# Modulation rows for all partitions: read back from a copy in DRAM instead of built by TensorE and ScalarE

## The chip, the cores and the metric

The kernel runs on one core of a Trainium2 chip. The metric is device microseconds from start to end of one execution. Engines are named as in the profile: PE is TensorE, DVE is VectorE, ACT is ScalarE, POOL is GpSimd and SP is SyncE. SP computes nothing here; it issues the weight loads.

## What is computed

Two layers of a diffusion backbone over 512 tokens of 1024 numbers: 256 context tokens and 256 latent tokens. Each layer is a mixer (a pooling part and differential attention, with a projection in and one out) and a mixture of experts (32 experts in 4 groups, two chosen in one group). Before each of the two, a token row is normalized and then modulated: multiplied by a scale row and shifted by a shift row. The result of each is multiplied by a gate row and added to the token. These rows come from a small product per layer, one set for each of the two streams (context and latent):

```python
def rmsnorm(x, g):
    xf = x.astype(jnp.float32)
    y = xf * lax.rsqrt(jnp.mean(xf * xf, axis=-1, keepdims=True) + EPS)
    return (y * g.astype(jnp.float32)).astype(x.dtype)

def modulate(h, shift, scale):
    return h * (1 + scale) + shift

def hier_moe(h, rc_w, rc_b, rf_w, rf_b, w_gate, w_up, w_down):
    ...
    logits_c = (t @ rc_w + rc_b).astype(jnp.float32)
    ...
    _, top_g = lax.top_k(logits_c, 1)
    ...
    top_v, top_i = lax.top_k(lf, TOP_K_FINE)
```

The routing is a top choice over logits, so the modulated rows are wanted at full 32-bit precision.

## The kernel before

**Tiles and parts.** The tokens are four tiles of 128 rows, one token per partition: tiles 0 and 1 are the context stream (stream 1), tiles 2 and 3 the latent stream (stream 0). The second layer needs only the latent tiles. In each layer the function that mixes runs first. It works through attention units (one tile and one head each: scores, softmax, values), and pooling, output products and the modulation for the experts are laid between. Then the experts run. Their weights are 1 MB loads that SP issues, into an arena of 19 slots of 1 MB, as slots become free.

**The modulation rows.** A layer's modulation rows are products of a conditioning vector with 1 MB weight blocks, "ada" units, summed in a PSUM tile `rowps`. When the last is there, `split_mod` (L430) adds the bias and multiplies by a gain, which gives one tile of 128 × 512: row 32·j + 2·cb + u holds one half (512 numbers) of one modulation vector for stream u. So every row lives in one partition, and the scaling of 128 tokens needs it in all 128. For this `split_mod` splits the tile into a high part `modh` (ACT, L436) and a low part `modl` (DVE, L437), which PE multiplies without loss.

**The broadcast.** `bcast` (L446) puts one unit per half row into the list `fillers`. A unit has two products, L454 with the high part and L455 with the low part, each with a left matrix that selects one row for all 128 columns, so that the row stands in every partition of PSUM; then ACT copies it out, L456. `bcast` is called for the gate rows of the mixer ("g1", tile `g`) at the start of the attention, and in `Moe.modulations` and `Moe.gain` for the experts' gate rows ("g2", also a tile `g`), scale rows ("A2", `ab[:, 0]`) and shift rows ("B2", `ab[:, 1]`). The tile `ab` holds one stream's rows; in the first layer it is filled for stream 1 (tiles 0 and 1) and filled again for stream 0.

**What sets the order.** Engines work in program order. `fill` and `spare` take units from the front of `fillers` between attention units while some time is to be filled; `drain(tag)` takes all up to the last with a tag, at the place where its result is needed: ahead of the first scaling (`half`, L1086), the norm (`norm`, L1108) and the sorting of the routed tokens (L1283). Behind the broadcasts, `fillers` holds the next layers' ada units. A tile's last steps (output product, scaling, transposes `turn`, routing `logits`, `norm`, `route`) stand in a lane with due times, made in `done` (about L869 to 884); `scaled_tile` (L894) holds the first tile of the new stream back until the last tile of the old one has gone through `norm`.

**Queues.** ACT issues its own transfers, in its own order: the pooling weights (`pw`, 256 KB, L671), the ada bias and gain (`modb`, L396 and L397), the normalized rows to DRAM (`hd`, L1125, 512 KB a tile). SP issues the weights. In the profile's queue table, q1 holds SP's transfers and q10 those of ACT.

Of the kernel before, what the change touches and what calls it, by code (L numbers as in the profile page):

```python
# [13 lines left out]
F32 = mybir.dt.float32  # L14
# [9 lines left out]
D = 1024  # L24
# [207 lines left out]
def backbone_kernel(ctx: ExitStack, tc: tile.TileContext, x, par_d, lam_d, modb_d, adaw, win, wout, wx, rw_d, pw_d, fg_d,  # L232
# [197 lines left out]
    def split_mod(l):  # L430
        m, g = gains.pop(l)
        tt(m, rowps.pop(l), m, op=OP.add)
        stt(m, m, cst[:, C_IND:C_IND + 1], g, op0=OP.add, op1=OP.mult)
        hi = consts.tile([128, 512], F32R, tag="modh", name=f"modh{l}")
        lo = consts.tile([128, 512], F32R, tag="modl", name=f"modl{l}")
        act.activation(hi, m, AF.Copy)  # L436
        tt(lo, m, hi.bitcast(F32), op=OP.subtract)  # L437
        mods[l] = (hi, lo)
        p = PS.get([128, 4, 128], F32, "shp")
        for k in range(4):  # L440
            pe.transpose(p.t[:, k], m[:, k * 128:k * 128 + 128], ident)
        shifts[l] = consts.tile([128, 4, 2, 2], F32, tag="shift", name=f"shift{l}")
        dve.tensor_copy(shifts[l], p.t[:, :, 64:128].rearrange("p k (h r) -> p k h r", h=2)[:, :, :, 2:4])
        p.free()

    def bcast(l, cb, j0, name, rows):  # L446

        for u, o in rows.items():
            for h in range(2):
                def f(u=u, h=h, o=o):  # L450
                    r = 32 * (j0 + h) + 2 * cb + u
                    p = PS.get([128, 512], F32, "bc")
                    sel = identr[:, r:r + 1].to_broadcast([128, 128])
                    pe.matmul(p.t, lhsT=sel, rhs=mods[l][0], start=True, stop=False)  # L454
                    pe.matmul(p.t, lhsT=sel, rhs=mods[l][1], start=False, stop=True)  # L455
                    act.activation(o[:, 512 * h:512 * h + 512], p.t, AF.Copy)  # L456
                    p.free()
                fillers.appendleft((("bc", l, name), 0.43, f))
                loaded[("bc", l, name)] = True


    def split(src, hi, lo, e=dve):
# [90 lines left out]
    def mixer(l, W3, rows, pre):  # L553
# [315 lines left out]
        def done(qt):  # L869

            i, n = qtiles.index(qt), len(qtiles) - 1
            lane = deque()
            units_of[qt] = 0
            if i == n:
                lane.append((2.6, 0, lambda: last_unit(qt, 0)))
                lane.append((3.1, 0, lambda: last_unit(qt, 1)))
            else:
                for nb in range(2):
                    lane.append((2.6, 2.5 * nb, lambda nb=nb: out_unit(qt, nb, 1, dve if i == n - 1 else gp)))
                lane.append((0, LAT if i == n - 1 else 3.2, lambda: scaled_tile(i)))  # L880
                lane.append((0.9, 1.3, lambda: (moe.turn(i, 0), moe.turn(i, 1))))
                lane.append((1.7, 0.5, lambda: moe.logits(i)))
                lane.append((0, 0, lambda: moe.route(i) if i == n - 1 else (moe.norm(i), moe.route(i))))
            lanes.append([clock[0], lane])

        def push():
# [6 lines left out]

        def scaled_tile(i):  # L894
            flush()
            while i and not last and stream(qtiles[i]) != stream(qtiles[i - 1]) and i - 1 not in moe.normed:
                push()
            for c in range(2):
                moe.half(i, c, dve if i == len(qtiles) - 2 else gp)
            moe.root(i)  # L900
# [134 lines left out]
    class Moe:  # L1035
        def __init__(self, l, tiles, gs, rw):
            self.l, self.tiles, self.gs = l, tiles, gs

            self.g2 = {0: gs.t[:, 1]} if l == NL - 1 else {u: gs.t[:, u] for u in range(2)}
            self.ab, self.normed = SB.get([128, 2, D], F32, "ab"), set()  # L1040
            self.T = len(tiles)
            self.nt, self.p, self.r = 128 * self.T, {}, {}

# [14 lines left out]
        def modulations(self):  # L1058
            l = self.l
            bcast(l, 2, 2, "g2", self.g2)  # L1060
            self.gain(stream(self.tiles[0]))
            n = sum(key == ("bc", l, "A2") for key, _, _ in fillers)
            fillers.insert(n, (("bc", l, "rb"), 2.0, self.bias))
            loaded["bc", l, "rb"] = True

        def gain(self, u):

            bcast(self.l, 1, 2, "B2", {u: self.ab.t[:, 1]})
            bcast(self.l, 2, 0, "A2", {u: self.ab.t[:, 0]})

        def bias(self):

# [13 lines left out]
        def half(self, i, c, e):  # L1086

            t, ns = self.tiles[i], slice(512 * c, 512 * c + 512)
            drain(("bc", self.l, "A2"))
            if c == 0:  # L1090
                self.r[i] = small([128, 2], tag="rq", bufs=4)
            act.activation(w2("t", BF, [128, 512]), X[:, t, ns], AF.Square, scale=D ** -0.5, accum_out=self.r[i][:, c:c + 1])
# [14 lines left out]

        def norm(self, i, aside=False):  # L1108
            t = self.tiles[i]
            drain(("bc", self.l, "B2"))  # L1110
            for c in (slice(0, 512), slice(512, 1024)):
                h, r, shift = self.rows[i][:, c], self.r[i][:, 0:1], self.ab.t[:, 1, c]
                if aside:
# [1 line left out]
                    gp.tensor_tensor(h, h, shift, op=OP.add)  # L1115
                else:
                    stt(h, h, r, shift, op0=OP.mult, op1=OP.add)
            self.normed.add(i)
            if i + 1 < self.T and stream(self.tiles[i + 1]) != stream(t):
                self.gain(stream(self.tiles[i + 1]))  # L1120
            if i < self.T - 2:
                self.send(i)

# [8 lines left out]

        def route(self, i):

            p = self.p.pop(i)
            lg, mc, m8 = self.lg[:, i], self.mc[:, i], self.m8[:, i]
            stt(lg, p.t[:, :40], self.r[i][:, 0:1], self.rb[:, stream(self.tiles[i])], op0=OP.mult, op1=OP.add)
# [38 lines left out]
        def run(self, next_loads=None, tail=None, at_end=None, again=None):  # L1176
# [103 lines left out]

            rank = tmp(T, 32)
            act.activation(rank, p.t[:, 0:T], AF.Copy)
            drain(("bc", l, "g2"))  # L1283
            key, junk, OHR = tmp(32), tmp(32), tmp(32)[0:32]
            keyc, rc, effc = (tmp(1)[0:32] for _ in range(3))
            pos = work.tile([1, 3, 32], I32, tag="pos", bufs=1, name=f"pos{l}")
# [593 lines left out]
```

## Time and profile before

| | us |
|---|---|
| runs | 976.27, 975.47, 969.62 (median 975.47) |
| the profiled execution | 968.64, its span 966.8 |
| PE busy | 813.3 (84% of the span) |
| DVE busy | 440.4 (46%) |
| ACT busy | 264.8 (27%) |
| POOL busy | 189.7 (20%) |
| DMA moved | 292.92 MB, mean 303 GB/s |

The busy shares are means over the span. The kernel has parts with different limits, so the strips of the page, which cut the span in 40 slices, have to be read beside them, and a change is weighed in the part in which it lies. Rows of the trace give a start in us, a duration in us (of a group of like instructions one behind the other, as x2, the whole), the engine, the line and the operation, with output and input; in brackets stands the idle time before it and what ended that.

### The profile page before, as it was taken

The numbers are of one execution on the slowest core, as the hardware profiler recorded it, in microseconds if no ns is written. First come the engines' busy times: TensorE is split into PE (matmuls) and PEld (weight loads), VectorE is DVE, ScalarE is ACT, GpSimd is POOL, SyncE is SP. The second block draws the span as 40 slices with busy tenths as digits, with TensorE's granted clock in tenths as the row PEclk, the third lists the DMA queues.
The fourth block names the chain that finished last, engine by engine and source line by source line (L and its number), as shares of the span: only waits on it lengthen the run. The fifth ranks groups of instructions, "written<-read, shape, count | busy, mean of one in ns | idle before, by whom it ended". The sixth has DMA issues, their size and how long they took to land. (4 is left out here: it accounts for less than half of the span.)

```text
span 966.8 us, 13398 instructions
## 1 busy us (share of the span) xinstructions
PE 813.3 (84%) x4825; PEld 438.1 (45%) x4825; DVE 440.4 (46%) x955; ACT 264.8 (27%) x592; POOL 189.7 (20%) x201
## 2 busy tenths in 40 slices
PE   4799999988996788989877765999879679997973
PEld 1467755555774233333211222687556534443311
DVE  0634405576476222222111169644575735767343
ACT  1622216345350111111000104632572311111101
POOL 1400002234611111111100024000126211222012
PEclk9799999998997899999997876899999789999987
DMA  9998397820729999997999992473237589999992
GB/s 378 416 364 314 128 355 309 324 88 7 297 99 365 368 402 416 416 417 303 415 419 418 408 403 102 172 287 131 98 106 274 237 334 418 417 419 415 367 420 93
DMA packets 49082, 292.92 MB, mean 303 GB/s; under 512 B 7571, under 2 KB 7955, under 8 KB 16880
## 3 DMA queue, kind: packets, MB, share of 16 engines
q1 hardware_dynamic: 36864, 265.74, 68.3%
q0 software_dynamic: 6336, 13.99, 3.7%
q10 hardware_dynamic: 5808, 12.25, 3.4%
q8 instruction: 42, 0.69, 0.3%
q14 instruction: 32, 0.26, 0.1%
HBM read 317.29 MB, written 15.30 MB: 344 GB/s over the span
## 5 line engine op out<-in xcount | busy, mean ns | idle before, releaser
L1479 PE MATMUL dn<-we,t 128*32 128x512 f32 (+2 forms) x672 | 106.7, 640 | 5.2 <-DMA we<-in_wx_dram 3.5
L1451 DVE SCALAR_TENSOR_TENSOR t<-t,tb,gu 128x256 f32<-128x256 f32 x25 | 12.0, 480 | 189.9 <-ACT t L1450 189.9
L1445 PE MATMUL gu<-we,hT0modl 128*32 128x512 f32 (+1 forms) x400 | 66.1, 625 | 9.3 <-DMA we<-in_wx_dram 8.7
L1450 ACT ACTIVATE t<-gu 128x256 f32<-128x256 f32 x25 | 9.6, 385 | 230.8 <-PE gu L1445 230.7
L1445 PE MATMUL gu<-we,hT0modh 128*32 128x512 f32 (+1 forms) x400 | 62.4, 623 | 8.8 <-DMA we<-in_wx_dram 6.8
L414 PE MATMUL rowps<-ada,sT 128*32 128x512 f32 x384 | 55.3, 667 | 4.8 <-DMA ada<-in_adaw_dram 4.8
L1479 PEld LDWEIGHTS dn<-we,t 128*32 128x32 f32 (+2 forms) x672 | 28.1, 122 | 65.8 <-issue 56.0
L1507 POOL TENSOR_TENSOR X<-X,m 128x512 f32<-128x512 f32 x24 | 30.7, 1278 | 130.3 <-DVE m L1505 130.1
L467 PE MATMUL pj<-hH,wh 128*128 128x512 f32 (+1 forms) x128 | 47.6, 372 | 0.0
L469 PE MATMUL pj<-hH,wl 128*128 128x512 f32 (+1 forms) x128 | 46.4, 363 | 0.0
L468 PE MATMUL pj<-hL,wh 128*128 128x512 f32 (+1 forms) x128 | 46.4, 363 | 0.0
L1445 PE MATMUL gu<-we,hT1modh 128*32 128x512 f32 (+1 forms) x272 | 41.3, 656 | 5.4 <-DVEq L1559 3.8
L1445 PE MATMUL gu<-we,hT1modl 128*32 128x512 f32 (+1 forms) x272 | 42.2, 632 | 3.6 <-DMA we<-in_wx_dram 3.6
L1507 DVE TENSOR_TENSOR X<-X,m 128x512 f32<-128x512 f32 x32 | 42.7, 1333 | 1.1
L718 ACT ACTIVATE e<-S,nb 128x512 f32<-128x512 f32 (+1 forms) x48 | 29.2, 613 | 46.7 <-DVE nb L715 31.4
L1445 PEld LDWEIGHTS gu<-we,hT0modl 128*32 128x32 f32 (+1 forms) x400 | 17.8, 120 | 52.9 <-issue 36.4
L1247 POOL DMA_INDIRECT h<-hd,ix x14 | 14.3, 1025 | 134.5 <-DVE iy L1254 61.6
L1445 PEld LDWEIGHTS gu<-we,hT0modh 128*32 128x32 f32 (+1 forms) x400 | 16.7, 119 | 50.2 <-issue 35.4
L712 DVE TENSOR_REDUCE mx<-S 128x1 f32<-128x512 f32 (+1 forms) x48 | 26.8, 596 | 27.5 <-PE S L710 27.4
L1505 DVE TENSOR_TENSOR m<-cb,g 128x512 f32<-128x512 f32 x56 | 36.5, 681 | 0.1
L751 PE MATMUL o<-v,t 128*128 128x128 f32 x160 | 25.4, 300 | 8.7 <-ACT t L739 8.7
L751 PEld LDWEIGHTS o<-v,t 128*128 128x128 f32 x160 | 21.0, 201 | 24.5 <-ACT t L739 21.9
(335 smaller groups left out, 1581.5 us busy)
## 6 DMA issues: line engine op xcount, KB each, us to landing
we<-in_wx_dram SPq DMA_DIRECT2D x207, 1024.0 KB
ada<-in_adaw_dram SPq DMA_DIRECT2D x48, 1024.0 KB
YD<-m ACTq DMA_DIRECT2D x1, 4096.0 KB
yb<-YD POOLq DMA_DIRECT2D x4, 1024.0 KB, 13.8
X<-in_x_dram SPq DMA_DIRECT2D x4, 512.0 KB
e<-in_modb_dram ACTq DMA_DIRECT2D x8, 256.0 KB
band<-in_band_dram SPq DMA_DIRECT2D x2, 1024.0 KB
hd<-h ACTq DMA_DIRECT2D x4, 512.0 KB
```

Of the source, the lines that this page charges most:

```text
L414: pe.matmul(rowps[l][32 * j:32 * j + 32], lhsT=sT[:, k, 4 - 2 * cb:36 - 2 * cb], rhs=h.t[:, 512 * j:512 * j + 512], start=cb < 2 and k == ...
L467: pe.matmul(ps, lhsT=lh, rhs=rh, start=first, stop=False)
L468: pe.matmul(ps, lhsT=lh, rhs=rl, start=False, stop=False)
L469: pe.matmul(ps, lhsT=ll, rhs=rh, start=False, stop=last)
L712: dve.reduce_max(mx[:, m:m + 1], p.t[:, :nk], axis=AX.X)
L718: act.activation(e[m][:, :nk], S[m].t[:, :nk], AF.Exp, scale=0.125, bias=nb[:, m:m + 1], accum_out=l_[:, m:m + 1])
L751: pe.matmul(o.t[:, h], lhsT=aT[:, kt], rhs=v.t[:, kt, h * 128:h * 128 + 128], start=kt == 0, stop=kt == n - 1)
L1247: gp.indirect_dma_start(out=hgs.t[:, g % 2], out_offset=None, in_=self.hd, in_offset=bass.IndirectOffsetOnAxis(ap=ix[:, :1], axis=0), boun ...
L1445: pe.matmul(p.t[r], lhsT=hT[k // 4][:, k % 4, r], rhs=gate_up(weights(w, k // 4), k), start=k == 0, stop=k == 7)
L1479: pe.matmul(ps[n2].t[r], lhsT=aT[:, k, r], rhs=down_w(weights(w, 2), k, n2), start=k == 0, stop=k == 1)
L1505: tt(m, q, self.g2[stream(t)][:, ns], op=OP.mult)
L1507: e.tensor_tensor(X[:, t, ns], X[:, t, ns], m, op=OP.add)
```

## The change

`split_mod` no longer splits. It writes the 128 × 512 tile as it is to a tile in DRAM, by a transfer that ACT issues. `bcast` no longer adds units to `fillers`: it issues at once, on ACT's queue, one transfer per stream that reads the two half rows from DRAM and repeats them for all 128 partitions (512 KB written to SBUF, read from 4 KB). There are 2 such writes, 256 KB each, and 12 such reads. What was drained from `fillers` for "A2", "B2" and "g2" goes. The refill of `ab` for the other stream, which `norm` called, is now a step of its own in the lane, behind `norm` and `route`; `scaled_tile` waits for it. The bias of the routing ("rb") goes to the front of `fillers` and is drained in `route`.

```diff
@@ split_mod
-        hi = consts.tile([128, 512], F32R, tag="modh", name=f"modh{l}")
-        lo = consts.tile([128, 512], F32R, tag="modl", name=f"modl{l}")
-        act.activation(hi, m, AF.Copy)
-        tt(lo, m, hi.bitcast(F32), op=OP.subtract)
-        mods[l] = (hi, lo)
+        mods[l] = dram.tile([128, 512], F32, name=f"mod{l}")
+        act.dma_start(mods[l], m)
@@ bcast
         for u, o in rows.items():
-            for h in range(2):
-                def f(u=u, h=h, o=o):
-                    r = 32 * (j0 + h) + 2 * cb + u
-                    p = PS.get([128, 512], F32, "bc")
-                    sel = identr[:, r:r + 1].to_broadcast([128, 128])
-                    pe.matmul(p.t, lhsT=sel, rhs=mods[l][0], start=True, stop=False)
-                    pe.matmul(p.t, lhsT=sel, rhs=mods[l][1], start=False, stop=True)
-                    act.activation(o[:, 512 * h:512 * h + 512], p.t, AF.Copy)
-                    p.free()
-                fillers.appendleft((("bc", l, name), 0.43, f))
-                loaded[("bc", l, name)] = True
+            r = 32 * j0 + 2 * cb + u
+            src = mods[l][r:r + 33:32]
+            act.dma_start(o.rearrange("p (h d) -> p h d", h=2), src[None].to_broadcast([128, 2, 512]))
@@ done
-                lane.append((0, 0, lambda: moe.route(i) if i == n - 1 else (moe.norm(i), moe.route(i))))
+                lane.append((0, 2.5, lambda: moe.route(i) if i == n - 1 else (moe.norm(i), moe.route(i))))
+                if stream(qtiles[i + 1]) != stream(qt):
+                    lane.append((0, 0, lambda: moe.gain(stream(qtiles[i + 1]))))
@@ scaled_tile
-            while i and not last and stream(qtiles[i]) != stream(qtiles[i - 1]) and i - 1 not in moe.normed:
+            while stream(qtiles[i]) not in moe.gained:
@@ Moe.modulations
-            n = sum(key == ("bc", l, "A2") for key, _, _ in fillers)
-            fillers.insert(n, (("bc", l, "rb"), 2.0, self.bias))
+            fillers.appendleft((("bc", l, "rb"), 2.0, self.bias))
@@ Moe.gain
+            self.gained.add(u)
+            bcast(self.l, 2, 0, "A2", {u: self.ab.t[:, 0]})
             bcast(self.l, 1, 2, "B2", {u: self.ab.t[:, 1]})
-            bcast(self.l, 2, 0, "A2", {u: self.ab.t[:, 0]})
@@ Moe.norm
-            self.normed.add(i)
-            if i + 1 < self.T and stream(self.tiles[i + 1]) != stream(t):
-                self.gain(stream(self.tiles[i + 1]))
```

How this moves instructions is seen on ACT at three places. The first is the start of the attention in the first layer, before the change: `modh` is the high part, `e` the exponentials of the first unit, `m` the copy of a pooling product, `wh` the split of an output weight, `g` the gate rows.

```order
L671 DMA o_954<-in_pw_dram 128x512 [waits DMAHW1_49]
L436 ACTIVATE modh_990<-e_554 128x512 [waits DVE_49]
L718 ACTIVATE e_1012,ls_1002<-S_1004,nb_1010 128x256 [waits DVE_49]
L718 ACTIVATE e_1014,ls_1002<-S_1007,nb_1010 128x256
L684 ACTIVATE m_1025<-pl_1016 128x512 [waits PE_49]
L463 ACTIVATE wh_1027<-('wout', 0)_59_931 128x512 [waits DMAHW6_49,DMAHW3_49,DMAHW2_49]
L463 ACTIVATE wh_1027<-('wout', 0)_59_931 128x512 x3
L456 ACTIVATE g_70_1001<-bc_1039 128x512 [waits DMAHW2_49,PE_49,Activation_49]
L456 ACTIVATE g_70_1001<-bc_1043 128x512 [waits PE_49]
```

The same place after the change (the lines are those of the changed kernel, some ten lower):

```order
L660 DMA o_954<-in_pw_dram 128x512 [waits DMAHW1_49]
L435 DMA mod_990<-e_554 128x512 [waits DMAHW3_49,DVE_49]
L448 DMA g_70_999<-mod_990 128x2x512 [waits DMAHW3_49,DMAHW2_49,DMAHW5_49,PE_49,Activation_49]
L448 DMA g_70_999<-mod_990 128x2x512 [waits DMAHW7_49]
L707 ACTIVATE e_1012,ls_1002<-S_1004,nb_1010 128x256 [waits DVE_49]
L707 ACTIVATE e_1014,ls_1002<-S_1007,nb_1010 128x256
L673 ACTIVATE m_1025<-pl_1016 128x512 [waits PE_49]
L452 ACTIVATE wh_1027<-('wout', 0)_59_931 128x512 [waits DMAHW6_49]
```

The write of the tile stands where the copy to the high part was; behind it are the two reads of the gate rows, of which the first waits for the write (DMAHW3), and only then the exponentials. The copies to `g` behind `wh` are gone.

The second place is the change of streams in the first layer, where tile 1 (context) is done and tile 2 (latent) is scaled. On ACT before the change, where `h2T` is a transposed tile, `hd` the rows in DRAM and `t` the squares of tile 2:

```order
L1105 ACTIVATE h2T_1783<-h2T_2082 128x512 [waits PE_49]
L456 ACTIVATE g_89_1774<-bc_2113 128x512 [waits DMAHW3_49,PE_49]
L456 ACTIVATE g_89_1774<-bc_2117 128x512 [waits PE_49]
L1125 DMA hd_1776<-h_91_1777 128x1024 [waits DMAHW6_49,DVE_49]
L456 ACTIVATE ab_1775<-bc_2139 128x512 [waits PE_49,Pool_49]
L456 ACTIVATE ab_1775<-bc_2143 128x512 [waits PE_49]
L1092 ACTIVATE t_2148,rq_2147<-X 128x512 [waits Activation_49]
```

And after it:

```order
L1095 ACTIVATE h2T_1767<-h2T_2054 128x512 [waits PE_49]
L1111 DMA hd_1760<-h_91_1761 128x1024 [waits DMAHW5_49,DVE_49]
L448 DMA ab_1759<-mod_990 128x2x512 [waits DMAHW7_49,Pool_49]
L448 DMA ab_1759<-mod_990 128x2x512 [waits DMAHW4_49,DMAHW0_49]
L1082 ACTIVATE t_2112,rq_2111<-X 128x512 [waits Activation_49]
```

Two reads, of the scale rows and of the shift rows, stand behind the send of the rows `hd`, in place of two copies from PSUM; the copies to `g` ahead of the send are gone, since those reads were issued before.

The third place is the start of the attention in the second layer, before the change:

```order
L671 DMA o_5513<-in_pw_dram 128x512
L436 ACTIVATE modh_5517<-e_5142 128x512 [waits DVE_49]
L718 ACT_TABLE_LOAD
L718 ACTIVATE e_5539,ls_5529<-S_5531,nb_5537 128x512 [waits DVE_49]
```

And after it:

```order
L660 DMA o_5455<-in_pw_dram 128x512
L435 DMA mod_5459<-e_5084 128x512 [waits DVE_49]
L448 DMA g_180_5468<-mod_5459 128x2x512 [waits DMAHW1_49,DMAHW0_49]
L707 ACT_TABLE_LOAD
L707 ACTIVATE e_5480,ls_5470<-S_5472,nb_5478 128x512 [waits DVE_49]
```

As in the first layer, the write stands in place of the copy, and the read that waits for it (DMAHW0) stands ahead of the table load and the first exponential.

## Rows read from the trace of the kernel before

**Rows 1.** The page: span, and PE and DMA busy tenths in 40 slices.

```profile
span 966.8 us, 13398 instructions
...
PE   4799999988996788989877765999879679997973
...
DMA  9998397820729999997999992473237589999992
```

**Rows 2.** Instructions of the tile bc: ns least/median/most, first to last start.

```profile
L454 PE MATMUL bc<-modh,identr x24: 387/397/792, 149.1 to 755.8; 128*128 128x512 f32 x24
...
L456 ACT ACTIVATE g<-bc x12: 578/603/626, 151.8 to 758.4; 128x512 f32<-128x512 f32 x12
```

**Rows 3.** Timeline, PE at 249 to 251 us: start, duration, engine, line.

```profile
249.64 0.40 PE L454 MATMUL bc<-modh,identr 128*128 128x512 f32 x1
...
250.56 0.39 PE L467 MATMUL wo<-wh,ch 128*128 128x512 f32 x1
```

**Rows 4.** Timeline, ACT behind a load's issue.

```profile
174.94 0.28 ACT L753 ACTIVATE t<-o 128x128 bf16<-128x128 f32 x1 [2.87 <-PE aT L737]
```

**Rows 5.** Timeline, ACT and PE, start of the first layer's attention.

```profile
146.02 0.63 ACT L436 ACTIVATE modh<-e 128x512 fp32r<-128x512 f32 x1 [4.71 <-DVE e L433]
...
148.36 0.47 ACT L718 ACTIVATE e<-S,nb 128x256 f32<-128x256 f32 x1 [1.71 <-DVE nb L715]
...
157.52 1.07 ACT L456 ACTIVATE g<-bc 128x512 f32<-128x512 f32 x2
...
157.92 1.10 PE L689 MATMUL pm<-m,o 128*128 128x512 f32 x2
```

**Rows 6.** Timeline, ACT's queue: the pooling load's issue in the first layer.

```profile
139.21 0.33 ACTq L671 DMA_DIRECT2D o<-in_pw_dram  x1
```

**Rows 7.** Queues of 142 to 147, then 146.5 to 147: packets, MB, share.

```profile
q1 hardware_dynamic: 245, 1.82, 86.8%
q10 hardware_dynamic: 142, 0.26, 13.7%
...
q10 hardware_dynamic: 1, 0.00, 1.1%
```

**Rows 8.** Windows: length, busy PE PEld DVE ACT POOL, granted clock, DMA share, GB/s.

```profile
148.00:158.00 10.00, 9.78 (x63) 7.34 (x62) 6.62 (x16) 7.66 (x19) 3.26 (x3) 1.00 0.97 393
158.00:160.00 2.00, 2.00 (x12) 0.40 (x11) 0.00 (x0) 2.00 (x8) 0.96 (x1) 1.00 0.11 41
```

**Rows 9.** Timeline, ACT's queue and DVE at the change of streams.

```profile
273.63 0.33 ACTq L1125 DMA_DIRECT2D hd<-h  x1
...
276.00 1.29 DVE L1093 TENSOR_TENSOR h<-X,ab 128x512 f32<-128x512 f32 x2
```

**Rows 10.** Queues of 274 to 277, then 950.5 to 953.

```profile
q10 hardware_dynamic: 144, 0.52, 43.1%
...
q10 hardware_dynamic: 143, 0.52, 58.4%
```

**Rows 11.** Timeline, ACT's queue and ACT, start of the second layer's attention.

```profile
684.99 0.35 ACTq L671 DMA_DIRECT2D o<-in_pw_dram  x1
...
686.12 1.28 ACT L718 ACT_TABLE_LOAD   x1
...
688.34 0.69 ACT L718 ACTIVATE e<-S,nb 128x512 f32<-128x512 f32 x1 [0.94 <-DVE nb L715]
```

**Rows 12.** Queue of ACT's transfers, 687 to 690.

```profile
q10 hardware_dynamic: 144, 0.26, 23.1%
```

**Rows 13.** Window of 692 to 696, columns as in rows 8.

```profile
692.00:696.00 4.00, 2.46 (x11) 1.26 (x10) 3.89 (x8) 1.52 (x4) 1.60 (x1) 1.00 0.19 37
```

**Rows 14.** Timeline, PE: the second layer's last routing logits.

```profile
757.13 1.98 PE L1131 MATMUL lg<-o,h2T 128*128 128x40 f32 x16 [0.75 <-ACT h2T L1105]
```

**Rows 15.** Window of 231 to 233, columns as in rows 8.

```profile
231.00:233.00 2.00, 1.25 (x6) 1.25 (x7) 2.00 (x2) 0.70 (x2) 1.68 (x2) 0.50 0.00 0
```

**Rows 16.** Timeline, PE at 231.75.

```profile
231.75 2.07 PE L751 MATMUL o<-v,t 128*128 128x128 f32 x8 [3.29 <-ACT t L739]
```

More of the change, by code (lines that the diff above doesn't have):

```diff
@@ L1039, in __init__ @@
             self.g2 = {0: gs.t[:, 1]} if l == NL - 1 else {u: gs.t[:, u] for u in range(2)}
-            self.ab, self.normed = SB.get([128, 2, D], F32, "ab"), set()
+            self.ab, self.gained = SB.get([128, 2, D], F32, "ab"), set()
             self.T = len(tiles)
@@ L1088, in half @@
             t, ns = self.tiles[i], slice(512 * c, 512 * c + 512)
-            drain(("bc", self.l, "A2"))
             if c == 0:
@@ L1109, in norm @@
             t = self.tiles[i]
-            drain(("bc", self.l, "B2"))
             for c in (slice(0, 512), slice(512, 1024)):
@@ L1133, in route @@
         def route(self, i):
+            drain(("bc", self.l, "rb"))
             p = self.p.pop(i)
@@ L1282, in run @@
             act.activation(rank, p.t[:, 0:T], AF.Copy)
-            drain(("bc", l, "g2"))
             key, junk, OHR = tmp(32), tmp(32), tmp(32)[0:32]
```

## The prediction

> **What bounds the kernel now.** I read the page first: its strips in 40 slices of 24.2 us show two layers, each in two parts [rows 1]. Counted from 0, the slices 4 to 11 and 25 to 31 (about 100 to 290 and 600 to 770 us) have PE mostly at 8 or 9 tenths and the DMA strip down to 0 to 3 in places: there the mixing of a layer runs, and its end is set by TensorE with ScalarE (ACT) and VectorE (DVE) taking turns. Where DMA stands at 9 (slices 12 to 23 and 33 to 38), expert weights stream in, and that part's length is bytes over rate. The stream starts when the routing is known, so a shift of the routing goes through to the end of its part nearly one for one; nothing in the stream takes it back. So the sum needs the two mixings only, and it counts what is on the way to the routing.
>
> The list of the tile's instructions gives what the change removes [rows 2]: 24 selection products of the high parts at 397 ns, 24 of the low parts of the same length, and 24 copies of 0.6 us on ACT, 12 into the gate rows (in the rows) and 12 into the scale and shift rows. The products overlap at their ends: from the first product at 249.64 to the next other product at 250.56 lie two pairs [rows 3]. So **a pair costs PE 0.46 us**, and all 24 cost 11.0 us. Sixteen pairs are in the first layer, eight in the second.
>
> **What the change adds.** ACT issues two writes of 256 KB and twelve reads of 512 KB, about 6.8 MB. At the stream's 416 GB/s that is 16 us of DMA time, nearly all in the slices where the DMA strip is low, so I count no bytes. Fourteen issues at 0.34 us are 4.8 us of ACT, against 14 us of copies gone. What counts is waiting: ACT works in order, and the first read must wait until the write has landed. Behind it are the softmax exponentials of the first attention units. The trace shows what that does: the ACT instruction at 174.94, behind a load's issue that had to wait, comes after 2.87 us of idle time, though what it reads was long there [rows 4].
>
> **Term a, first layer, the round trip: +4.4 us.** The write goes out where the copy to the high part was, at 146.02; the first exponential runs now at 148.36 [rows 5]. How long does the write take? The nearest transfer is the 256 KB load of the pooling weights, in rows of 2 KB on the same queue beside the same weight loads: issued at 139.21, it had all but its last packet through by 146.5, and that one in 146.5 to 147 [rows 6, 7]. Its share of the queue in 142 to 147 was 0.26 MB against 1.82 MB of the loads' queue. So 7.2 us: the write lands at 153.2, two read issues bring 153.9, and the exponential starts 5.5 us late. The two gate copies (1.07 us a pair of them, at 157.52) no longer lie in ACT's way, which leaves 4.4, and PE's second mixing product (157.92) moves to about 162. PE was busy 9.78 of 10 us in 148 to 158 [rows 8], so it has no slack to take this up; two weight products that the filler list now puts there only move work ahead. Bounds: 0, if the write lands as fast as on an idle queue (below), and +10.7, if it lands only when the loads ahead are through, at 158 to 160 [rows 8].
>
> The Trainium skill (DMA: Bandwidth & Descriptors, section "Two DMAs through the same engine are not ordered") says that a transfer that reads what an earlier one writes is not safe by the queue's order alone. Here the order shows the wait that follows from this, on ACT.
>
> **Term b, four gate pairs there: −1.84 us** (4 × 0.46), since PE is full in that stretch [rows 8].
>
> **Term c, four pairs of the context rows: −1.84 us.** Two stand at 249.64 [rows 3] and two ahead of the first norm, PE full at both (9 tenths in slice 10). Their reads go out where the filler list was filled, in slice 9 (218 to 242), whose DMA digit is 0, and are wanted after 250, so they are hidden.
>
> **Term d, the change of streams: 0 us.** Four pairs just ahead of the third tile's scaling and four behind it go, 8 × 0.46 = 3.7 us. In their place ACT issues two reads behind the write of the normalized rows. Those reads refill the buffer that the norm has just read. The send goes out at 273.63 now, and the scaling, DVE at 276.00, needs the new scale rows [rows 9]. The send's 0.52 MB pass in 274 to 277, and the one row broadcast to all partitions at the end has its 0.52 MB in a window of 2.5 us [rows 10]. With the send ahead, and a 1 MB expert load that now starts there too, I put the scale rows at 279: a wait of 3 us against 3.7 us saved, of which a part lies behind other waits. I take 0, with bounds −2.2 (rows in 1.3 us) and +2 (rows in 5 us).
>
> **First layer: +4.4 − 1.84 − 1.84 + 0 = +0.7 us.**
>
> **Term e, second layer, the round trip: +4.4 us.** The write is issued at 685.0 right behind the pooling load (684.99), whose 0.26 MB pass in 687 to 690 [rows 11, 12]. I let the write land one microsecond behind it, 691.0; the read's issue takes 0.35, the table load 1.28, and the first exponential starts at 692.6 instead of 688.34 [rows 11]. Bounds: +1.3 (landing in 2.6 us) and +6.
>
> **Term f, the layer's first four pairs: 0 us.** They fill stretches where PE waits for the softmax; in 692 to 696 it was busy 2.46 of 4 us [rows 13]. Without that cover they are worth 4 × 0.46 = 1.84 us.
>
> **Term g, its last four pairs: −2.2 us.** The last of them is at 755.8 [rows 2], straight ahead of the routing logits, which start at 757.13 after 0.75 us of waiting for a copy that ACT makes behind the broadcast copies [rows 14]. Four pairs are 1.84, and I add half of the 0.75. Their reads are issued some 30 us before. Bounds −3 and 0.
>
> **Second layer: +2.2 us. The sum: +2.9, say +3 us.** The profiled execution took 968.64 us with a span of 966.8 [rows 1]; the sum gives 971.6. The median of the runs shown is 6.8 us above the profiled one (their spread is 6.7), so on it I forecast 975.47 + 3 = **978.5 us**.
>
> **The rivals.** *Cheap round trips (0.12).* If the write lands within 2.6 us, as the 0.52 MB at 274 or the broadcast row do on an idle queue [rows 10], term a is 0 and term e +1.3; the sum is 0 − 3.7 + 0 + 1.3 − 2.2 = −4.6 us: 964.0, on the median 970.9. Against it: the load at 139.21 took near three times that [rows 6, 7], and the second layer has a load issued beside it.
>
> The Trainium skill (same page, section "Anatomy of one DMA — SWDGE (gpsimd) path") gives a fit of 2.0 us and the bytes over 436 GB/s; for 256 KB an estimate of 2.6 us, for which the sum would be that rival's −4.6. The load at 139.21 disagrees, as it had loads beside it.
>
> *All pairs count, all trips hidden (0.07).* The faster side: all 24 pairs lie on PE's path and nothing waits: −11.0 us, 957.6, on the median 964.4, which is −1.1%. For it: PE is at 9 tenths in the first mixing. Against it: ACT's order puts the exponentials behind the write.
>
> *The write is kept behind the weight loads (0.14).* The other side: if its bytes pass only when the loads ahead are through, near 159.5 (their rate falls to 41 GB/s in 158 to 160 [rows 8]), term a grows by 6.3 us. PE would then stand idle for longer than 3 us. Behind such a wait, of 3.29 us, the trace shows a granted clock of 0.50 in 231 to 233, 1.2 GHz, the lower of its two levels [rows 15, 16]; if that lasts some 6 us, as an estimate three times this window, it costs 3 us more. The sum is +12 us: 980.9, on the median 987.8, +1.3%. It decides from a landing after about 157. Against it: the pooling load got 0.26 MB through in 142 to 147 beside a full queue [rows 7].
>
> *The change does less than it says* (that the products are still there) is excluded by the order: no product of that tile is left.
>
> **How the numbers follow.** The forecast has 0.67, the rivals 0.12, 0.07 and 0.14. The forecast's own range is the sum of its terms' likely halves, −3 to +8 around +3: 972 to 984. The range that leaves out no more than 2 in 10 takes in the cheap rival and the slower one: 967 to 988. A measurement of this kernel can tell about 1% from no change, 9.8 us. Faster by more than that is the all-pairs rival, 0.07; slower is the last rival and a little of the forecast's upper end, 0.15; the rest, 0.78, is within 1%.
>
> **What would show it.** Terms a and e: the idle time ahead of the first exponential in each layer, which I expect near 153.9 and 692.6, and the bytes of the second queue in 146 to 153. Terms b, c, g: the gaps between neighbouring products where the pairs stood. Term d: an idle time of about 3 us on DVE ahead of the scaling of the third tile. The time at which the two streams of expert loads begin gives each layer's sum. The forecast is wrong if the write lands at once or after 157, or if the reads at the change of streams take more than 5 us.

## The result, and the profile after

The changed kernel is slower: 999.04 us median of 4 runs (995.71 to 1002.07) against 973.41 (969.62 to 976.27). The ratio is 1.0274, with a 95% interval of 1.024 to 1.0307, so some 26 us were lost where 3 were forecast. Its profiled execution, the fastest of the four, took 995.71 us, and its span is 27.1 us above that in [rows 1]:

```profile
span 993.9 us, 13295 instructions
...
PE 811.8 (82%) x4777; PEld 442.6 (45%) x4777; DVE 438.9 (44%) x953; ACT 252.0 (25%) x566; POOL 189.7 (19%) x201
...
PE   4799998887986879989776764999677779998883
...
PEclk9799998998985989999989876999889879999997
DMA  9988399712855899997999992563328579999892
...
q10 hardware_dynamic: 9360, 19.06, 5.9%
```

On this page (span, busy us, strips by 40 slices of now 24.8 us, ACT's DMA queue with packets, MB, share) the products and copies are gone. Yet PE's busy time fell by 1.5 us only (813.3 before), though 11 us of products went: what remains runs longer, at a lower mean clock (0.906 in this execution, 0.920 to 0.935 in the timed executions of the kernel before). ACT's queue moves 19.06 MB; the strip of the DMA shows room for it in the mixings.

Where the time went is read by putting marks of the program side by side. All differences are in us against the kernel before (its own times in the second column), from the start times of the timeline. The last two columns are experiments told below (e_g1 moves the waiting read, e_all makes four moves at once):

| mark | before | after | e_g1 | e_all |
|---|---|---|---|---|
| first layer, first exponential | 148.36 | +6.68 | +0.36 | −0.24 |
| last product with the values | 254.83 | +6.39 | −0.69 | −3.05 |
| third tile's scaling (DVE) | 276.00 | +14.11 | +6.22 | −1.92 |
| first table of the experts | 297.04 | +15.03 | +7.21 | −3.06 |
| second layer, modulation rows (DVE) | 680.07 | +15.98 | +11.01 | −1.90 |
| first exponential | 688.34 | +20.68 | +10.67 | −2.24 |
| last product with the values | 726.52 | +27.21 | +14.24 | −1.73 |
| first table of the experts | 768.50 | +26.99 | +13.71 | −2.23 |

So 15 us were lost in the first mixing and 11 in the second (26.99 − 15.98), and the expert streams gave back nothing, as forecast. One caution for the marks behind the first stream: from the first table of the experts to the second layer's modulation rows the profiles of this study take between 383.0 and 386.8 us (383.0 before, 384.0 after, 386.8 in e_g1), and no run says why. There are four places. The first is the start of the attention. The timeline of the changed kernel, to be read beside [rows 5] and [rows 11]:

```profile
146.57 0.34 ACTq L435 DMA_DIRECT2D mod<-e  x1
...
154.08 0.91 ACTq L448 DMA_DIRECT2D g<-mod  x2
155.04 0.47 ACT L707 ACTIVATE e<-S,nb 128x256 f32<-128x256 f32 x1 [13.19 <-issue]
...
156.60 2.08 PE L678 MATMUL pm<-m,o 128*128 128x512 f32 x2 [3.32 <-ACT m L673]
...
701.37 0.44 ACTq L435 DMA_DIRECT2D mod<-e  x1
...
707.31 0.38 ACTq L448 DMA_DIRECT2D g<-mod  x1
707.72 1.28 ACT L707 ACT_TABLE_LOAD   x1 [6.15 <-DMA mod<-e]
709.02 0.69 ACT L707 ACTIVATE e<-S,nb 128x512 f32<-128x512 f32 x1
...
710.79 1.22 PE L678 MATMUL pm<-m,o 128*128 128x256 f32 x2 [5.31 <-ACT m L673]
```

From the write's issue to the read's lie 7.5 us in the first layer and 5.9 in the second, all of it ACT standing still, and PE runs dry behind it for 3.3 and 5.3 us. The second and third places are a block of reads at 240 us and the refill of the scale rows at the change of streams, to be read beside [rows 9]; the fourth is the routing bias `rb` in the second layer:

```profile
240.79 2.02 ACTq L448 DMA_DIRECT2D ab<-mod  x2
...
242.86 1.67 ACT L452 ACTIVATE wh<-('wout', 0)_78_1206 128x512 fp32r<-128x512 f32 x3 [1.94 <-PE rowps L414]
...
245.58 1.23 PE L740 MATMUL o<-v,t 128*128 128x128 f32 x8 [3.26 <-ACT t L728]
...
282.99 1.27 ACTq L448 DMA_DIRECT2D ab<-mod  x2
...
290.11 1.29 DVE L1083 TENSOR_TENSOR h<-X,ab 128x512 f32<-128x512 f32 x2 [3.57 <-DMA ab<-mod]
...
293.60 0.63 PE L1094 MATMUL h2T<-cst,h 128*128 128x128 f32 x4 [3.90 <-DVE h L1083]
...
746.59 0.73 PE L1067 MATMUL rb<-o,shift 128*2 128x40 f32 x16 [2.59 <-DMA o<-in_rw_dram]
```

Behind each of these waits PE's granted clock is at the lower of its two levels, or near it as a mean over the window. The windows of the changed kernel, with the columns of rows 8 (the granted clock is the third number from the right); the one in [rows 8] for 148 to 158 shows 1.00. The window of 271 to 277 lies behind the same bias in the first layer, where PE stood idle for 2.14 us at 270.53:

```profile
156.00:158.00 2.00, 1.40 (x2) 0.50 (x2) 0.38 (x1) 2.00 (x6) 0.85 (x1) 0.50 0.89 284
158.00:161.00 3.00, 3.00 (x11) 0.71 (x12) 3.00 (x4) 0.62 (x2) 2.10 (x2) 0.50 0.65 218
246.00:250.00 4.00, 4.00 (x15) 3.26 (x14) 3.89 (x8) 0.37 (x2) 1.06 (x2) 0.57 0.83 189
271.00:277.00 6.00, 6.00 (x16) 4.66 (x17) 2.14 (x12) 0.00 (x0) 1.37 (x3) 0.50 0.46 188
296.00:300.00 4.00, 3.86 (x18) 3.86 (x19) 0.12 (x1) 0.58 (x2) 0.56 (x2) 0.50 1.01 420
711.00:714.00 3.00, 3.00 (x7) 0.85 (x7) 2.19 (x2) 1.81 (x4) 2.67 (x2) 0.50 0.06 17
718.00:728.00 10.00, 9.96 (x34) 7.25 (x36) 4.79 (x11) 7.03 (x20) 2.18 (x3) 0.51 0.40 145
748.00:752.00 4.00, 3.70 (x18) 3.62 (x18) 0.53 (x4) 0.53 (x3) 0.00 (x0) 0.57 0.94 153
```

From this, **theory 1**: the loss is waits of ACT, DVE and PE on the new transfers and on the moved bias, with the low clock that they leave. **Theory 2**: it is the 6.8 MB more on the DMA queues. **Theory 3**: the products had covered PE's gaps, and without them PE falls dry and slow whatever ACT does.

### The profile page after: what moved, and what is told of

Read it like the earlier page. It is cut to its first block, busy times and chain, and to the rows that moved or that the text cites. A ratio compares the mean times of both kernels' runs of the same rounds, so it can differ in the third digit from the quotient of the medians.

```text
span 993.9 us, 13295 instructions
## 1 busy us (share of the span) xinstructions
PE 811.8 (82%) x4777; PEld 442.6 (45%) x4777; DVE 438.9 (44%) x953; ACT 252.0 (25%) x566; POOL 189.7 (19%) x201
## 3 DMA queue, kind: packets, MB, share of 16 engines
q10 hardware_dynamic: 9360, 19.06, 5.9%
## 5 line engine op out<-in xcount | busy, mean ns | idle before, releaser
L1431 PE MATMUL gu<-we,hT0modh 128*32 128x512 f32 (+1 forms) x400 | 65.1, 648 | 12.2 <-DMA we<-in_wx_dram 9.3
L1431 PE MATMUL gu<-we,hT0modl 128*32 128x512 f32 (+1 forms) x400 | 61.6, 594 | 8.8 <-DMA we<-in_wx_dram 8.2
```

Of the source, the lines that this page charges most:

```text
L1431: pe.matmul(p.t[r], lhsT=hT[k // 4][:, k % 4, r], rhs=gate_up(weights(w, k // 4), k), start=k == 0, stop=k == 7)
```

## The experiments

Times are medians; in each group of runs the kernel before was timed beside them on the same chip (971.0 to 972.8 us), and a gain is told against the changed kernel by the distance to that (25.6 us for the changed kernel itself). Four runs each leave such a difference uncertain by some 4 us, so a single gain of 3 or 4 us is at the edge of what the times tell; for these the trace has to show that the wait is gone, and e_all that the gains add up.

### e_g1: the waiting read behind the first units

```diff
-        bcast(l, 1, 0, "g1", {0: g1.t[:, 0]} if last else {u: g1.t[:, u] for u in range(2)})
...
+        bcast(l, 1, 0, "g1", {0: g1.t[:, 0]} if last else {u: g1.t[:, u] for u in range(2)})
         for i in range(N):
             turned(i)
```

> The changed kernel with one move: the two (second layer: one) reads of the mixer's gate rows are issued after the first three attention units instead of right behind the write, so that ACT does not stand behind the write. Theory 1 (the added time is waits of ACT and VectorE on the new transfers, each of which leaves PE idle for over 3 us and then at half clock): the start of the attention recovers 3 to 4 us in the first layer and 7 to 8 us in the second (round trip 4.7, half clock 3), so about 988 us where the changed kernel took 999.0; first exponentials near 149 and 8.3 us behind the modulation rows of the second layer, as before the change. Theory 2 (7 MB more on the DMA rings): no transfer is less, so it stays at 999. Theory 3 (without the products PE has nothing to cover its gaps): PE still falls to half clock there; 996 at best.

Measured: 982.36 us, ratio 1.0095 (1.0068 to 1.0123). The distance fell from 25.6 to 9.6 us, so this one wait, with what it leaves behind it, was worth **16 us**, more than expected. The first exponential is back, with the wait on VectorE that it had before, and PE's second product too:

```profile
148.72 0.47 ACT L707 ACTIVATE e<-S,nb 128x256 f32<-128x256 f32 x1 [7.05 <-DVE nb L704]
...
157.42 1.10 PE L678 MATMUL pm<-m,o 128*128 128x512 f32 x2
```

By the table the first layer's marks gain 7.8 us (15.03 − 7.21 at the table of the experts) and the second layer's own part falls from 11.0 to 2.7 (13.71 − 11.01). Of the first gain 5.0 us are left at the second layer's modulation rows, since the stream between was longer in this execution. Theory 2 is out for this part, since no byte less is moved, and so is theory 3's bound of 996.

### e_rb: the routing bias back

The drain goes back behind the first logits. `fresh`, set when a layer's experts are set up, keeps `spare` from taking the bias right behind the issue of the load that it reads.

```diff
 def logits(self, i):
...
+            drain(("bc", self.l, "rb"))
 def route(self, i):
...
-            drain(("bc", self.l, "rb"))
...
 def spare():
...
+            elif moe and moe.fresh:
+                moe.fresh = False
```

> The changed kernel with the routing bias (ten-number products 'rb') back where it stood relative to its neighbours: behind the logits of the first tile in the first layer, and not in the first free place behind its own weights' load in the second. Theory 1: in the second layer PE no longer waits 2.6 us for that load nor runs at half clock after it (3.6 us); in the first layer PE no longer waits behind VectorE's norm at 268 to 271 us (about 3 us); together 992 to 993 us against 999.0. Theory 2 and theory 3: no change, 998 to 1000, since the same work is done with the same transfers.

Measured: 994.33 us, ratio 1.0212 (1.0189 to 1.0234), 4 us won. In the second layer it is as expected: between the first and the last product with the values the changed kernel lost 4.94 us, here 1.31, and the bias runs without a wait:

```profile
752.40 0.73 PE L1069 MATMUL rb<-o,shift 128*2 128x40 f32 x16
```

In the first layer nothing was won, though PE's wait of 2.14 us for the bias is down to 0.28. I had expected 3 us. From the last product with the values to the first table of the experts, the stretch in which the bias lies, it takes 50.86 us against 50.85 in the changed kernel. All marks start 1.7 us later in this execution, where the write took 7.7 us.

### e_ab: the scale rows refilled early

```diff
                 lane.append((0, LAT if i == n - 1 else 3.2, lambda: scaled_tile(i)))
+                if stream(qtiles[i + 1]) != stream(qt):
+                    lane.append((0, 0, lambda: moe.scales(stream(qtiles[i + 1]))))
...
+            if u == stream(self.tiles[0]):
+                self.scales(u)
...
```

`scales` holds the read of the scale rows (A2) alone; the read of the shift rows (B2) stays where it was.

> The changed kernel with the refill of the scale rows for the second stream issued right after the last scaling of the first stream, before that tile's transposes; the shift rows' refill stays behind the norm. Theory 1: VectorE's wait of 3.6 us ahead of the third tile's scaling goes, with PE's 3.9 us of idle time behind it and its half clock: 993 to 995 us against 999.0. Theory 2: nothing is won, 999, as the same bytes move at nearly the same time. Theory 3: 997 to 999.

Measured: 995.53 us, ratio 1.0232 (1.0208 to 1.0257), 3 us won. The scaling no longer waits for a transfer:

```profile
278.00 0.37 ACTq L448 DMA_DIRECT2D ab<-mod  x1
...
283.26 0.40 ACTq L448 DMA_DIRECT2D ab<-mod  x1
286.71 1.29 DVE L1090 TENSOR_TENSOR h<-X,ab 128x512 f32<-128x512 f32 x2
```

From the last product with the values to the table of the experts the lag now grows from +6.61 to +9.99 us, where it grew from +6.39 to +15.03: 5 us less in the first layer. At the second layer's modulation rows 3 of them are left (+12.88 against +15.98).

### e_g2: two reads less at 240

```diff
 def modulations(self):
...
-            bcast(l, 2, 2, "g2", self.g2)
...
             act.activation(rank, p.t[:, 0:T], AF.Copy)
+            bcast(l, 2, 2, "g2", self.g2)
```

> The changed kernel with the reads of the experts' gate rows taken out of the block of four reads at 240 us (three at 744) and issued when the routing's ranks are copied. Theory 1: ACT's copies of the output weights no longer come 1.9 us late at 241 to 243, PE's idle time of 3.3 us at 245 falls under 2 and its half clock to 250 goes: 995 to 996 us against 999.0, unless the late reads collide with the first expert loads. Theory 2: 999. Theory 3: 997 to 999.

Measured: 994.52 us, ratio 1.0214 (1.0187 to 1.0241), 4 us won (the interval of this one alone reaches from 1 to 6 us against the changed kernel's 1.0274, and that has its own of ±3 us). The wait that was to go is gone, 0.30 instead of 3.26 us:

```profile
242.94 0.45 ACTq L448 DMA_DIRECT2D ab<-mod  x1
243.43 0.48 ACTq L448 DMA_DIRECT2D ab<-mod  x1
244.06 2.19 ACT L452 ACTIVATE wh<-('wout', 0)_78_1206 128x512 fp32r<-128x512 f32 x4
...
246.79 1.16 PE L740 MATMUL o<-v,t 128*128 128x128 f32 x8 [0.30 <-ACT t L728]
```

The gain is in the marks too: from the first to the last product with the values of the first layer it takes 87.56 us, against 91.10 in the changed kernel. The profiled execution is the slowest of the four even so (999.25 us; the others 992.62 to 996.28); where it lost time is told under e_warm2.

### e_all: the four together

> The changed kernel with all four moves at once (gate reads of the mixer late, routing bias back, scale rows refilled early, experts' gate reads late). All bytes and all DMA issues of the change remain, all 48 products are gone. Theory 1 (waits, and the half clock they leave behind): the four single gains add up, 16.7 + 4.7 + 3.5 + 4.5 = 29 us on 999.0, so 968 to 974 us, level with the kernel before (972.8). Theory 2 (traffic): the 16 us that 6.8 MB take at 416 GB/s are still there; 985 or more. Theory 3 (PE's gaps uncovered without the products): the gains overlap, 976 to 982, and more time at half clock than in the kernel before.

Measured: 971.72 us beside 972.24, ratio 0.9998 (0.9972 to 1.0024). The four single gains are 16 + 4 + 3 + 4 = 27 us, and together they take back the whole loss. Theory 2 is out: the kernel moves the same bytes as the changed one,

```profile
span 966.2 us, 13298 instructions
...
PE 798.6 (83%) x4777; PEld 431.5 (45%) x4777; DVE 440.8 (46%) x953; ACT 252.0 (26%) x566; POOL 190.4 (20%) x201
```

with all 9360 packets of ACT's queue. Theory 3 is out in its main claim, as no product came back and PE is busy 14.7 us less than before. A remainder of it stands: taking the products out was worth little. With these four waits gone the marks gain 3.1 us in the first mixing and 0.3 in the second (2.23 − 1.90), where 11 us of PE time were removed. The execution's end gains 0.6 us. These are net gains, as the fourteen transfers are still issued.

### e_warm and e_warm2: useless products in PE's gaps

```diff
         scores(1)
         pool_a(1)
+        p = PS.get([128, 512], F32, "bc")
+        for k in range((3, 5)[l]):
+            pe.matmul(p.t, lhsT=u.t[:, 2, 0:128], rhs=band.t[:, 0:512], start=True, stop=True)
+        p.free()
         pool_b(0)
```

This is e_warm2; e_warm has (14, 22) in its place.

> The changed kernel with useless products added on PE, nothing else: 14 in the first layer and 22 in the second (128 x 512 each, full-clock spacing 0.23 us, so 3.2 and 5.1 us), where PE stands idle behind ACT's wait for the write (3.3 us at 153, 5.3 us at 705). Their result is read by nobody. Theory 1 in its part on the clock: the waits stay, but the stretches at granted clock 0.50 behind them (154 to 160, 707 to 713) shrink, and the kernel gets 4 to 6 us faster by doing more, 993 to 995 us. If the loss is the waits alone: 999 to 1002, as the products fill idle time at best.

> The changed kernel with useless products on PE at the same two places as in e_warm, but sized by what one took there (two passes, 0.88 us, since its operands are not rounded): 3 in the first layer and 5 in the second, 2.6 and 4.4 us, a little less than PE's idle time behind ACT's wait (3.3 and 5.3 us). Theory 1 in its part on the clock: the waits stay, the stretches at granted clock 0.50 behind them shrink, and the kernel gets 4 to 6 us faster, 993 to 995 us against 999.0. If the loss is the waits alone: 999 to 1001.

Measured: e_warm 1007.85 us, ratio 1.0351 (1.0309 to 1.0393). It is mis-sized: one product on these operands takes two passes, 0.88 us and not 0.23, so it says little. e_warm2 took 999.81, ratio 1.0286 (1.0254 to 1.0318), which is no gain. The reason is in its trace:

```profile
156.00:158.00 2.00, 2.00 (x12) 0.40 (x12) 1.09 (x1) 1.92 (x4) 1.56 (x2) 1.00 0.97 312
...
161.00:168.00 7.00, 6.54 (x26) 3.84 (x26) 2.22 (x8) 5.32 (x14) 1.27 (x1) 0.56 1.00 383
```

```profile
161.46 2.87 PE L669 MATMUL pl<-band,u 128*128 128x128 f32 x13 [2.81 <-ACT e L707]
...
721.44 1.79 PE L669 MATMUL pl<-band,u 128*128 128x128 f32 x8 [4.54 <-ACT e L707]
```

The clock behind the first gap is 1.00, as meant. But PE then runs into the next wait for ACT, 2.8 and 4.5 us, and the low clock of the first layer comes at 161 instead of 154. It was moved there and not removed, and where it came it cost time. From the first exponential to the first product with the values (155.04 to 170.12 in the changed kernel) it takes 19.02 us here and 15.08 there. The run e_g2, whose program is the changed kernel's up to 240 us, shows the same without a useless product. PE's wait is nearly the same (3.44 us against 3.32), but the low clock lasts to 168 and not to 161, and the stretch takes 18.97 us. The window of 161 to 168, first in the changed kernel, then in e_g2:

```profile
161.00:168.00 7.00, 7.00 (x52) 4.46 (x48) 4.43 (x14) 5.59 (x15) 2.27 (x2) 0.99 0.90 344
...
161.00:168.00 7.00, 7.00 (x26) 4.01 (x26) 2.19 (x8) 5.36 (x14) 1.43 (x2) 0.50 0.98 386
```

PE has no gap in either, and does half the products at half the clock: **3.9 us** for the longer low clock, the one difference that the rows show there. Over the four executions of the changed kernel the mean clock falls as the time grows (0.906 at 995.71 us, 0.903 at 998.17, 0.898 at 999.92 and at 1002.07). In the second layer of e_warm2 the low stretch (718 to 728 in the changed kernel) shrinks, and the part from the modulation rows to the last product with the values goes from 57.7 to 55.3 us, before 46.5. So both halves of theory 1 have a price. Of the low clock's, 2.4 us were got back in the second layer; in the first it changes by 3.9 us from one execution to the next. The wait alone was not measured apart from it.

### b_g1 and b_rb: one part of the change alone, in the kernel before

```diff
# b_g1
         mods[l] = (hi, lo)
+        copies[l] = dram.tile([128, 512], F32, name=f"mod{l}")
+        act.dma_start(copies[l], m)
...
-        bcast(l, 1, 0, "g1", {0: g1.t[:, 0]} if last else {u: g1.t[:, u] for u in range(2)})
+        for u_, o in ({0: g1.t[:, 0]} if last else {u: g1.t[:, u] for u in range(2)}).items():
+            src = copies[l][2 + u_:2 + u_ + 33:32]
+            act.dma_start(o.rearrange("p (h d) -> p h d", h=2), src[None].to_broadcast([128, 2, 512]))
# b_rb
-            fillers.insert(n, (("bc", l, "rb"), 2.0, self.bias))
+            fillers.appendleft((("bc", l, "rb"), 2.0, self.bias))
...
+            drain(("bc", self.l, "rb"))
```

> The kernel before with one part of the change alone: the modulation tile is also written to DRAM, and the mixer's gate rows (4 half rows in the first layer, 2 in the second) come by reads of it on ACT's queue at the place where the change has them; all other rows still come by products. By theory 1 (ACT held behind the write) nearly the whole of the e_g1 difference appears: 8 us in each layer less some 2 us for the six pairs that go, 984 to 988 us where the kernel before takes 971 to 973. If the cost of that wait arises only together with the other parts of the change (PE's gaps uncovered): under 980.

> The kernel before with the routing bias put at the front of the filler list as in the change, all else as before. In the second layer it is then the first thing that PE takes after the routing weights' load is issued, and PE waits for that load. By theory 1: 3 to 4 us slower, 975 to 976 us, all of it between the last softmax and the first routing of the second layer; nothing in the first layer. If the 3.6 us seen there came from the missing products instead: no change, 971 to 973.

Measured: b_g1 982.13 us beside 971.58, ratio 1.0104 (1.0076 to 1.0131), 10.6 us slower. That is under the 12 to 16 expected and over theory 3's bound: the waiting read does its harm with all other products in place, and a part of the 16 us of e_g1 seems to arise only with the rest of the change. In its profiled execution (986.77 us) the first exponential is 8.3 us late in the first layer, and in the second 4.7 us counted from the modulation rows, as in the changed kernel. How the other 5 us of e_g1 come about was not tried; the low clock, whose price changes from one execution to the next, is a candidate.

b_rb 974.76 us, ratio 1.0027 (1.0009 to 1.0045), 3.2 us slower, as theory 1 has it. In its second layer PE waits for the routing weights' load in the kernel with all products:

```profile
725.56 0.73 PE L1075 MATMUL rb<-o,shift 128*2 128x40 f32 x16 [2.48 <-DMA o<-in_rw_dram]
```

Between the first and the last product with the values (702.50 and 726.52 in the kernel before) it loses 3.2 us (5.92 − 2.73), and nothing behind.

### e_pw: one step further

e_all shows one wait that the products had hidden, PE on the pooling weights at 689:

```profile
689.08 0.78 PE L678 MATMUL pm<-m,o 128*128 128x256 f32 x2 [1.48 <-DMA o<-in_pw_dram]
```

```diff
             wh, wl = Ws.popleft()
+            if n == len(halves) - 1:
+                pw = w2("o").rearrange("p (g e) -> p g e", g=4)
+                act.dma_start(pw, pw_d[l].rearrange("p (g e) -> p g e", g=4))
...
-        pw = w2("o").rearrange("p (g e) -> p g e", g=4)
-        act.dma_start(pw, pw_d[l].rearrange("p (g e) -> p g e", g=4))
```

> e_all with one more move: the pooling weights' load (256 KB, on ACT's queue) is issued ahead of the last half of the projection instead of behind it. In e_all PE waits 1.5 us for that load at 689 in the second layer, now that no products stand ahead of it, and runs at half clock to 699. By theory 1 both go: 2 to 4 us under e_all, 967 to 970 us where the kernel before takes 972; if the half clock there has another cause, 970 to 971.5.

Measured: 969.33 us beside 971.0, ratio 0.9981 (0.9963 to 1.0000). It is the fastest kernel of the study, by 1.7 us against the kernel before, at the edge of what the interval tells. Beside e_all, which was 0.5 us under its own kernel before, that is 1.2 us and not the 2 to 4 expected. The wait of 1.48 us is gone (0.28 at 687.74), but PE arrives at the next wait for ACT that much earlier, as in e_warm2:

```profile
687.74 0.70 PE L679 MATMUL pm<-m,o 128*128 128x256 f32 x2 [0.28 <-ACT m L674]
...
694.99 1.22 PE L679 MATMUL pm<-m,o 128*128 128x256 f32 x2 [4.49 <-ACT m L674]
```

The mark at the last product with the values is that of e_all (−1.88 against −1.73), so the mechanism expected is not shown; what was won shows in the expert part (−1.4 against −0.6 at the end of the span), where this move changes nothing. Its cause stays open.

## Why the prediction was wrong

The forecast was 978.5 us with a range to 988; 999 lies outside, on the side of the rival that had 0.14, and 11 us beyond its price. Step by step:

**What bounds the kernel**: right in the main. The shifts of the mixing went through the expert streams with little change (15.0 at the first table, 16.0 at the next layer's start, 27.0 at the second table and 27.2 at the end); in the experiments up to 4 us were lost in the first stream.

**Terms a and e, the round trips**: the latency was right (7.5 us against 7.2 forecast; the second first exponential 4.70 us late against 4.4, the first 6.7 against 5.5). (Its own figures give 4.3 for term e and put the load that it takes as a measure at 7.3 to 7.8 us, and by the reckoning of its upper bound the lower one of term d is −1.7; none of this matters.) The step that failed is the price. It took the delay of the first exponential as the whole cost, and ACT as one queue with one head. By e_g1 the two waits cost 16 us, not 8.8; alone in the kernel before (b_g1) they cost 10.6, with six pairs gone. The delays of the two first exponentials make 11.4 of the 16. Of the rest, 2.4 us are the low clock in the second layer (e_warm2), and in the first an execution in which it lasts longer loses 3.9 more (e_g2). Behind the head stood also the copies of pooling products that PE waits for and the splits of output weights that ACT and DVE make; what they add is read from the order and was not tried apart. The rival priced this kind of thing, idle PE and a low clock of some 6 us, but tied it to a late landing (beyond 157), which did not come: it landed at 154.

**Terms b, c, d and g, the pairs**: mis-sized, and by nearly as much. Twenty pairs were counted at 0.46 us on the path, 9.6 us with the copies' wait; e_all shows that all of them with their copies are worth 3.4. For term b the stretch from the first exponential to the first product with the values tells it: 16.43 us before and 15.57 in e_all, 0.86 won where 1.84 were counted. PE was busy 9.78 of 10 us in 148 to 158 [rows 8], and 10.00 of 10 in e_all without the pairs. The calls there take units from `fillers` for a given time (0.9 us), and in place of two pairs they took a unit of weight products of 1.06 us, at 148.91 and at 153.38 in e_all. So the freed time went to other work of the list, and that this work was then done earlier was worth little too; that a busy PE there ran ahead of ACT and DVE is argued from this. The all-pairs rival (0.07) fell with this.

**Term c, the reads at 240**: the transfers are hidden, as forecast, but their issues are not. The 0.34 us of an issue was taken for all; the last two of five in a row took 2.02 us of ACT, and PE's 3.26 us of idle time follows. e_g2 shows it, 4 us by the times and 3.5 by the marks.

**Term d, the change of streams**: the rows were to be there 5.4 us after the send's issue; they took 7.5 (282.56 to 290.11). The send and both reads share ACT's queue, which may be why; no run parts them. Its row of the changed kernel for 283 to 290.2 us (packets, MB, share):

```profile
q10 hardware_dynamic: 572, 1.37, 74.2%
```

That is 190 GB/s, with 0.10 MB of other queues beside it. The wait was 3.6 us, near the 3 said, but the 3.7 us of pairs that it was set off against were not there. e_ab wins 3 us at the end and 5 in the layer.

**What no step held**: the place of the routing bias. The diff moves it to the front of the fillers, right behind the issue of the load that it reads. e_rb and b_rb give 4 and 3.2 us for it, by the marks in the second layer.

Put together, as an estimate from these differences: 7 us of round trips, 6 of pairs, 4 of reads at 240 and 4 of the bias are 21 of the 23 us by which the sum fell short.

**Signs named ahead**: the first exponentials (153.9 and 692.6 named, 155.04 and 709.02 seen, the latter 4.70 late in its layer), the second queue's bytes between 146 and 153, and DVE's wait of 3 us (3.57) all came. They confirmed the mechanism and said nothing of its price. One of the signs named for a wrong forecast came too: the reads at the change of streams took over 5 us, 7.1 from the issue at 282.99 to the scaling.

## What to carry to other kernels

A transfer that an in-order engine waits for costs that engine's whole queue, so issue the dependent read where its data is wanted, behind the work that does not need it: that alone was 16 of 26 us here, and no byte was saved. When PE work is taken out, ask what will stand in its place and which engine PE will wait for next; in a stretch with a busy share of 98% products of 1.84 us were worth 0.86. And follow each step that a diff moves to the front of a list back to the load that it reads.

## What the runs showed of the hardware

The issue of a transfer on ACT is not a fixed cost. Most of the reads that repeat a row for all partitions took 0.4 to 0.5 us; the second behind a send took 0.79 (283.48), and the fifth transfer in a row 1.5 to 1.9. In e_g1, ACT's queue, second and last read of that block:

```profile
234.45 0.48 ACTq L448 DMA_DIRECT2D g<-mod  x1
...
235.49 1.82 ACTq L448 DMA_DIRECT2D ab<-mod  x1
```

With two reads less in the block (e_g2) each took under 0.5 us. What the fifth waits for no run here shows.

What a low granted clock of PE costs depends on where it falls. With PE busy without a gap from 161 to 168, it cost 3.9 us (e_g2 against the changed kernel, whose programs are the same there). Where PE waits for ACT anyway it cost next to nothing: e_pw shortened a low stretch (690 to 699 in e_all, 693 to 699 there), and the marks behind it moved by 0.15 us. How long it lasts is not fixed by the program: behind nearly the same wait it ended at 161 in one execution and at 168 in the other.
